# Log-softmax over 8192 rows of 50000: a loop of 62 rounds over eight buffers in place of straight code

## The chip, the cores and the metric

One core of a Trainium2 chip. The metric is the device time of one execution in microseconds (us). "Before" is the kernel given, "changed" the one after the edit. Executions come in a fast and, now and then, a slow state; fast ones are compared with fast ones.

## The reference

```python
x: (16, 512, 50000) float32
max_x   = max(x, axis=-1)
shifted = x - max_x
out     = shifted - log(sum(exp(shifted), axis=-1))
```

Each element is read once and written once: 1638.4 MB in, 1638.4 MB out.

## The kernel before

A tile is 16 rows of the input. Each row is cut into 8 pieces, so that a tile fills 128 partitions with 6250 elements each (3.2 MB); there are 512 tiles. Eight tile buffers of 25000 bytes per partition lie in SBUF, the on-chip memory. Python unrolls everything: the program is one straight line of 512 copies.

```python
G = 8; R = P // G; EXP_C = 3125; NBUF = 8; AHEAD = 7

data = ctx.enter_context(tc.tile_pool(name="data", bufs=NBUF))
...
def load(t):
    buf = data.tile([P, W], FP32, name="buf")
    nc.sync.dma_start(out=buf, in_=xt[t])              # issued from SP
    tiles[t] = buf

def front(t):
    nc.vector.reduce_max(out=pmax, in_=buf, axis=AX)   # DVE, 6.7 us
    ...                                                # DVE: maximum across the 8 pieces, 4 short ops
    for j in range(nexp):                              # ACT: two exponentials with row sums
        nc.scalar.activation(out=dump, in_=buf[:, j * EXP_C : (j + 1) * EXP_C],
            func=ACT.Exp, bias=negmax[:, 0:1], scale=1.0, accum_out=part[:, j : j + 1])
    for j in range(nexp):                              # PE: sum across the 8 pieces
        nc.tensor.matmul(rowsum, ones, part[:, j : j + 1], start=j == 0, stop=j == nexp - 1)
    nc.scalar.activation(out=logsum, in_=rowsum, func=ACT.Ln)

def back(t):
    nc.vector.tensor_scalar(out=buf, in0=buf, scalar1=shift.pop(t)[:, 0:1],
        scalar2=logs.pop(t), op0=ALU.add, op1=ALU.subtract)     # DVE, 3.5 us
    nc.scalar.dma_start(out=ot[t], in_=buf)            # issued from ACT

for t in range(AHEAD):
    load(t)
for t in range(ntiles + 1):
    if t < ntiles:
        front(t)
    if t >= 1:
        back(t - 1)
    if t + AHEAD < ntiles:
        load(t + AHEAD)                                # waits for the store that frees the buffer
```

## Time and profile before

| | before |
|---|---|
| time, median of 3 (lowest, highest) | 7614.08 us (7613.85, 7614.22) |
| data moved | 432 GB/s in nearly every slice |
| DVE / ACT / PE busy | 73% / 41% / 8% |
| load, issue to landing | 51.9 us |
| store, issue to landing | 37.5 us |
| instruction fetch packets on the page | 68 + 16 |

The page of a profile has the busy share of each engine in 40 slices of the span, a row DMA with the share of the 16 DMA engines, and a row GB/s. A line of a group gives the source line, the engine, the operation, what it writes and reads, the count, then the busy time and mean, then the idle time before it and who ended it. The prediction below shows these lines.

### The profile page before, as it was taken

How to read it: one execution, taken by the hardware profiler on the slowest of the kernel's cores; microseconds unless marked ns; L12 is line 12 of the kernel's file. 1: busy time of each engine (PE TensorE's matmuls, PEld its weight loads, DVE VectorE, ACT ScalarE, POOL GpSimd, SP SyncE). 2: the span in 40 equal slices, each digit the busy share in tenths (PEclk: the TensorE clock that was granted, in tenths of full speed). 3: DMA queues.
4: the chain of work that ended last, by engine and by line, in shares of the span. 5: the costliest groups of instructions: out<-in, count | busy, mean ns of one | idle time of the engine just before them, and what ended most of it. 6: DMA issues, size and time to landing. Idle time of an engine off the chain costs nothing.

```text
span 7612.6 us, 12833 instructions
## 1 busy us (share of the span) xinstructions
PE 600.6 (8%) x2048; PEld 513.2 (7%) x2048; DVE 5567.2 (73%) x3072; ACT 3153.1 (41%) x2561; POOL 1.2 (0%) x7
## 2 busy tenths in 40 slices
PE   0000000000000000000000000000000000000000
PEld 0000000000000000000000000000000000000000
DVE  7777777777777777777777777777777777777776
ACT  4444444444444444444444444444444444444443
POOL 0000000000000000000000000000000000000000
DMA  9999999999999999999999999999999999999998
GB/s 425 433 432 432 432 432 432 432 432 432 432 432 432 432 432 432 432 432 432 432 432 432 432 432 432 432 432 432 432 432 432 432 432 432 431 432 432 432 432 380
DMA packets 147540, 3277.68 MB, mean 431 GB/s; under 512 B 16384, under 2 KB 16384, under 8 KB 16384
## 3 DMA queue, kind: packets, MB, share of 16 engines
q1 hardware_dynamic: 73728, 1638.43, 50.0%
q10 hardware_dynamic: 73728, 1638.43, 50.0%
q14 instruction: 68, 0.56, 0.0%
q8 instruction: 16, 0.26, 0.0%
HBM read 1638.40 MB, written 1638.40 MB: 430 GB/s over the span
## 4 chain that ended last, share of the span: by engine, by line
DVE 73%; another core or an unknown queue 25%; issue 1%; DMA 0%; ACT 0%; PE 0%; ACTq 0%
DVE pmax L81 45%; DVE buf L117 23%; DVE allmax L84 1%; DVE rowmax L86 1%; DVE spread L91 1%; DVE negmax L96 0%; DMA buf<-in_x_dram 0%; ACT dump L102 0%; PE rowsum L108 0%; ACT logsum L112 0%; ACTq L102 0%
## 5 line engine op out<-in xcount | busy, mean ns | idle before, releaser
L81 DVE TENSOR_REDUCE pmax<-buf 128x1 f32<-128x6250 f32 x512 | 3411.8, 6664 | 1953.7 <-DMA buf<-in_x_dram 1953.7
L102 ACT ACTIVATE dump<-buf,negmax 128x3125 f32<-128x3125 f32 x1024 | 2938.1, 2869 | 4092.9 <-DVE negmax L96 4029.5
L117 DVE TENSOR_SCALAR buf<-buf,negmax,logsum 128x6250 f32<-128x6250 f32 x512 | 1789.7, 3496 | 4.5 <-ACT logsum L112 3.6
L108 PE MATMUL rowsum<-part,ones 128*128 128x1 f32 x2048 | 600.6, 363 | 6991.7 <-ACT dump L102 6991.7
L108 PEld LDWEIGHTS rowsum<-part,ones 128*128 128x128 f32 x2048 | 513.2, 311 | 7079.0 <-ACT dump L102 7057.2
L112 ACT ACTIVATE logsum<-rowsum 128x1 f32<-128x1 f32 x512 | 87.6, 171 | 345.8 <-PE rowsum L108 345.8
L102 ACT ACTIVATION_READ_ACCUMULATOR dump<-buf,negmax 128x1 f32 x1024 | 191.1, 187 | 0.0
L96 DVE STREAM_TRANSPOSE negmax<-spread 128x32 f32<-128x32 f32 x512 | 108.2, 211 | 17.7
L84 DVE STREAM_TRANSPOSE allmax<-pmax 128x32 f32<-128x32 f32 x512 | 108.3, 211 | 17.4
L86 DVE TENSOR_REDUCE rowmax<-allmax 128x4 f32<-128x32 f32 x512 | 95.3, 186 | 17.7
L91 DVE COPY spread<-rowmax 128x32 f32<-128x32 f32 x512 | 92.9, 181 | 17.8
L67 ACT ACT_TABLE_LOAD x1 | 1.3, 1283 | 0.8 <-PEq L146 0.8
L59 POOL TENSOR_SCALAR_AFFINE_SELECT ones<-ones 128x128 f32<-128x128 f32 x1 | 0.4, 403 | 0.1
L63 POOL TENSOR_SCALAR_AFFINE_SELECT ones<-ones 128x128 f32<-128x128 f32 x1 | 0.4, 397 | 0.1
L57 POOL MEMSET ones<- 128x128 f32 x1 | 0.2, 204 | 0.3 <-POOLq L146 0.3
L146 POOL MEMSET const-bfloat16-1.0<- 128x1 bf16 x1 | 0.1, 101 | 0.0
L146 POOL MEMSET const-uint8-127<- 128x1 uint8 x1 | 0.1, 101 | 0.0
L146 POOL MEMSET const-float32-0.0<- 128x1 f32 x1 | 0.1, 98 | 0.3 <-issue 0.3
L146 POOL MEMSET const-float32-1.0<- 128x1 f32 x1 | 0.1, 98 | 0.0
## 6 DMA issues: line engine op xcount, KB each, us to landing
buf<-in_x_dram SPq DMA_DIRECT2D x512, 3125.0 KB, 51.9
out_dram<-buf ACTq DMA_DIRECT2D x512, 3125.0 KB, 37.5
```

The costliest lines, as they stand in the source:

```text
L59: nc.gpsimd.affine_select(out=ones3, in_=ones3, pattern=[[-G, R], [0, G]], base=0, channel_multiplier=1, compare_op=ALU.is_ge, fill=0.0,)
L63: nc.gpsimd.affine_select(out=ones3, in_=ones3, pattern=[[G, R], [0, G]], base=G - 1, channel_multiplier=-1, compare_op=ALU.is_ge, fill=0.0,)
L67: nc.scalar.preload_act_table_set("natural_log_exp_and_others")
L81: nc.vector.reduce_max(out=pmax, in_=buf, axis=AX)
L84: nc.vector.transpose(out=allmax, in_=pmax.to_broadcast([P, SQ]))
L86: nc.vector.tensor_reduce(out=rowmax, in_=allmax.rearrange("p (r g) -> p r g", g=G), op=ALU.max, axis=AX, negate=True,)
L91: nc.vector.tensor_copy(out=spread.rearrange("p (r g) -> p r g", g=G), in_=rowmax[:, :, None].to_broadcast([P, SQ // G, G]),)
L96: nc.vector.transpose(out=negmax, in_=spread)
L102: nc.scalar.activation(out=dump, in_=buf[:, j * EXP_C : (j + 1) * EXP_C], func=ACT.Exp, bias=negmax[:, 0:1], scale=1.0, accum_out=part[:, ...
L108: nc.tensor.matmul(rowsum, ones, part[:, j : j + 1], start=j == 0, stop=j == nexp - 1)
L112: nc.scalar.activation(out=logsum, in_=rowsum, func=ACT.Ln)
L117: nc.vector.tensor_scalar(out=buf, in0=buf, scalar1=shift.pop(t)[:, 0:1], scalar2=logs.pop(t), op0=ALU.add, op1=ALU.subtract,)
```

## The change

The intent is a short program: one body of eight tiles that runs 62 times, between a first and a last round of straight code. The loop is built without a barrier at the end of each round (`iteration_sync="reg_based"`: the waits compare against counts kept in registers). Since the row numbers are then in registers, the compiler can no longer see that stores touch different rows, so this is declared.

```diff
-    for t in range(AHEAD):
-        load(t)
-    for t in range(ntiles + 1):
-        if t < ntiles:
-            front(t)
-        if t >= 1:
-            back(t - 1)
-        if t + AHEAD < ntiles:
-            load(t + AHEAD)
+    bufs = [data.tile([P, W], FP32, name=f"buf{j}") for j in range(NBUF)]
...
+    def back(j, t, queue=nc.scalar):
...
+        store = queue.dma_start(out=dram(ot, t), in_=buf).ins
+        tc.add_to_no_dep_group("stores", store)
+        tc.declare_no_dep(
+            store, group="stores", across_iterations=True,
+            reason="each tile's rows of the output are written once",
+        )
+
+    def round_of(t, first=False, last=False):
+        for j in range(NBUF):
+            front(j)
+            if first and j == 0:
+                continue
+            back((j - 1) % NBUF, t + j - 1)
+            if j == 0 or not last:
+                load((j - 1) % NBUF, t + j - 1 + NBUF)
+
+    for j in range(NBUF):
+        load(j, j)
+    round_of(0, first=True)
+    with tc.For_i(NBUF, ntiles - NBUF, NBUF, iteration_sync="reg_based") as t:
+        with tc.manual_schedule():
+            round_of(t)
+    round_of(ntiles - NBUF, last=True)
+    back(NBUF - 1, ntiles - 1, queue=nc.sync)
```

(Cut: the pools' sizes, an assertion, and the small tiles, which get fixed names in place of rotating ones: eight each of `negmax` and `logsum`, one for each buffer, two of `part`, one of the others.)

## The prediction

> **What bounds the kernel now.** I read the page's head and slices first, then the DMA queues, the waits, the groups, and last the two ends of the run in stretches.
>
> The slices and the queues:
>
> ```profile
> span 7612.6 us, 12833 instructions
> DMA  9999999999999999999999999999999999999998
> GB/s 425 433 432 432 432 432 432 432 432 432 432 432 432 432 432 432 432 432 432 432 432 432 432 432 432 432 432 432 432 432 432 432 432 432 431 432 432 432 432 380
> ...
> q1 hardware_dynamic: 73728, 1638.43, 50.0%
> q10 hardware_dynamic: 73728, 1638.43, 50.0%
> q14 instruction: 68, 0.56, 0.0%
> q8 instruction: 16, 0.26, 0.0%
> ```
>
> The reader sees a flat 432 GB/s from end to end, half loads and half stores, and two small queues of instruction fetches. No slice has a hole. The groups and waits say that the engines follow the transfers:
>
> ```profile
> L81 DVE TENSOR_REDUCE pmax<-buf 128x1 f32<-128x6250 f32 x512 | 3411.8, 6664 | 1953.7 <-DMA buf<-in_x_dram 1953.7
> L117 DVE TENSOR_SCALAR buf<-buf,negmax,logsum 128x6250 f32<-128x6250 f32 x512 | 1789.7, 3496 | 4.5 <-ACT logsum L112 3.6
> ...
> buf<-in_x_dram SPq DMA_DIRECT2D x512, 3125.0 KB, 51.9
> out_dram<-buf ACTq DMA_DIRECT2D x512, 3125.0 KB, 37.5
> ...
> SPq L75 <- DMA out_dram<-buf: 7305.6, 504, 26.8
> ```
>
> The fullest engine, DVE, works 5567.2 us of 7612.6, 10.87 us in each of 512 tiles, and waits 1953.7 / 507 = 3.9 us a tile for a load. A load's issue waits about 14.5 us (7305.6 / 504) for the store that frees its buffer. So eight buffers go round: 51.9 us to land, some 29 us in the engines, 37.5 us to store, together 8 tiles of 14.85 us. At any time 51.9 + 37.5 = 89.4 us of round trip are in flight; 89.4 / 14.85 = 6.0 tile transfers of 7.4 us each, some 44 us of queued work per DMA engine.
>
> In the single packet records one 25000-byte packet follows the other on an engine every 924.7 ns, and each engine has 8192 of them: 8192 x 0.9247 = 7575 us. The completion writes add 1024 x 0.006 = 6 us. 7581 us is what no order of the same transfers can undercut. The first packet starts about 2.5 us into the span, and some 2 us follow the last, so the floor is about 7586 us. The kernel is 27 us, 0.35%, above it. Where those are shows in stretches of the run:
>
> ```profile
> 3000.00:4000.00 1000.00, 79.20 (x270) 67.68 (x270) 731.05 (x403) 413.36 (x338) 0.00 (x0) 1.00 1.00 432
> ...
> 7535.00:7580.00 45.00, 4.70 (x16) 4.01 (x16) 33.07 (x19) 23.62 (x20) 0.00 (x0) 1.00 0.76 327
> 7580.00:7613.00 33.00, 1.17 (x4) 1.00 (x4) 12.44 (x7) 6.16 (x5) 0.00 (x0) 1.00 0.66 282
> ```
>
> (The last three columns are clock, DMA share and GB/s.) DMA is full in the middle and idle for 0.24 x 45 + 0.34 x 33 = 22 us in the last 77. The semaphore records say why. A tile's 16 increments, one per DMA engine, land within 2 us of each other at the start, but within 32.6 us for the last loads of the steady part, growing evenly; 13 engines are done with their loads 40 us before the last three. So three engines fall behind little by little, a load counts as landed when the slowest has it, and in the tail the others have nothing left.
>
> I looked for what delays them. Around each fetch packet in 3000 to 3260 us the packet chain of one engine slips: by 0.31 us for the fetch itself and about 0.3 us one packet later (small queue q14), by 0.92 and 0.4 us (q8). 62 x 0.63 + 16 x 1.33 is about 60 us. That is the size of three engines behind by some 20 us each, and PE, ACT and DVE are the three large instruction streams. I can't name the DMA engines in the records, so this match is an inference.
>
> **What the Trainium skill says.** (1) "DMA: Bandwidth & Descriptors", section "Where 436 GB/s comes from", puts the ceiling at 435.2 GB/s, from 16 ports. The trace agrees: 432, that is 99.3% of it. (2) The same page, "Why a DMA increments its semaphore by 16 and not by 1": the 16 parts finish independently, and only the full count means landed. The trace agrees, with spreads from 2 to 32.6 us. (3) "Runtime: NRT & Kernel Launch", "Instruction fetch mechanics": instructions stream in blocks by DMA, prefetch is sequential, and a taken branch whose target is outside the two blocks held stalls for a fetch. This trace shows blocks of 16384 bytes (16 in q8, which fits PE's 4096 instructions) and of 8192 bytes (62 in the body of q14); it has no branch to show the rest. (4) "Advanced Engine Details and Errata", "Control Flow Timing": a branch takes about 51 ns, a compare-and-branch about 108 ns. No run yet shows it.
>
> **The change part by part.**
>
> *Buffers and order.* Still eight buffers, and load t+8 still waits for store t, as before in another notation. Eight loads stand in front instead of seven, but before issued its eighth with nothing to wait for as well. Small tiles go from four copies to one; all but one are made and read on DVE alone, in order, and the partial sums keep two copies, read by PE within a microsecond. Cost 0.
>
> *Instructions.* The work of a tile is the same: DVE 6 instructions, ACT 5 and an issue, PE 8, SP an issue. A round of eight tiles adds a branch and register steps per engine. If each wait and each DMA address costs three such steps at 0.1 us (the skill's compare-and-branch as an estimate), DVE with some 3 waits a tile gets 8 x 3 x 0.3 = 7 us a round, against a slack of 8 x 3.9 = 31 us. ACT is 41% busy and has 70 us of slack in a round of 119; SP has nearly all of it. On the path: 0.
>
> *The back edge.* If an engine stalls there for a fetch, I estimate under 10 us: the fetch queues behind data packets of 0.93 us. A stall of S starves the DMA engines only when it outlasts the queued work, 44 us evenly shared, and it is made up from 31 us of slack before the next. A barrier would have needed everything drained; this loop has none. On the path: 0.
>
> *Stores declared independent.* In straight code the compiler sees that stores touch different rows. In a loop their addresses are in registers, so without the declaration each could wait for the one before, 37.5 us from issue to landing against 14.85 us of a tile. With it, stores keep two or three in flight as now. Against the kernel before: 0.
>
> *Fetches.* Straight code fetches each block once: 78 in the steady run. A round holds about 48 instructions on DVE and on ACT, 64 on PE, plus waits and register steps. That should fit in the blocks held, and nearly all fetches disappear. Then the engines stay level, the last load lands earlier by what the slowest engine was late, some 20 us (24 us by another count: the tile takes 14.857 us where 16 packets and two completion writes take 14.81, times 512). The 34.5 us after that landing (7578.0 to 7612.6: maximum, exponentials, last two stores) stay. Stores pushed into the tail give some back; the floor of 7586 also stands in the way. I take 17 us: 7614 - 17 = 7597.
>
> *Tail.* The last store goes out on SP instead of ACT. It waits for the same DVE write, then for the DMA engines. Under 1 us.
>
> **The rivals.**
> 1. *The loop refetches its blocks each round*, since the body crosses a block border or a prefetch of the next block throws out the target. Then 62 rounds x 1 or 2 fetches x 0.63 us = 39 to 78 us on the DMA engine concerned, where there were about 15 to 20. It falls behind faster, and once the queue's 44 us are used up its own total sets the time: plus 20 to 65 us, 7630 to 7680. For it: waits and register steps could double the body, and the skill's account of sequential prefetch. Against it: 48 to 64 instructions are well below a block.
> 2. *The lag is not due to fetches* but belongs to three slower DMA engines. Then nothing moves: 7610 to 7616. Against it: the spacing of packets is 924.7 ns on all of them, with no slower group.
> 3. *The loop's waits are coarser than the straight code's*: loads or stores that wait for an older transfer on the same semaphore (there are eight DMA semaphores for six transfers in flight), or for all of an earlier round. Two transfers fewer in flight would be hidden, since 44 us are queued where a few are needed; a complete drain each round would cost a refill of some 40 us x 62 = 2500 us. The words "without barriers" speak against it.
> 4. *DVE becomes the bound*: it needs 4 us more a tile, 32 us a round. No counted cost comes near.
>
> **Range and chances.** Base case 7597 at about 0.55; no change, 7613, at 0.2; refetching at 0.15; coarser waits at 0.1, mostly above 7680. The weighted middle is about 7602 us. Eight times in ten between 7585, the floor, and 7650. Faster by 2% would be 7462, below the floor of 7586: 0.01, for an error of mine in that floor. Slower by 2% is over 7766, only through rival 3: 0.06. Within 2%: 0.93.
>
> **What would show it.** Right: 432 GB/s in every slice, the same DVE wait of about 3.9 us a tile for loads, instruction packets down from 84 to some 30 or fewer, the landing spread of loads near 2 to 10 us up to the end, and less idle DMA in the last 77 us. Rival 1: instruction packets in the hundreds. Rival 2: few instruction packets, but a spread that still grows to 30 us. Rival 3: DMA below 9 in the slices at regular distances, SP waiting for loads or ACT's queue for stores. What would make me wrong most: holes in the DMA row once a round.

## The result, and the profile after

The changed kernel takes 7645.64 us in the median of 6 runs, five of them from 7644.98 to 7646.1 (median 7645.45) and one slow one of 7816.88; before took 7614.15 beside it. The ratio of the fast runs is 1.0041 (95% interval 1.0028 to 1.0054). Ratios here are the mean time of one kernel's fast runs over that of the other's of the same rounds, so not quite the ratio of the medians quoted. That is 31 us slower: inside the range and within 2%, but on the other side of 7614 from the base case of 7597.

The only profile of this first set fell into the slow execution. It shows 432 GB/s up to about 5250 us and about 403 from there on; that is not explained here and nothing rests on it. The profile below is of the first experiment, the same kernel once more, in a fast run of 7645.29 us.

Page of the changed kernel, slices and queues:

```profile
span 7643.6 us, 21938 instructions
...
DMA  9999999999999999999999999999999999999997
GB/s 423 433 431 433 431 433 431 433 431 433 431 433 431 431 432 432 432 432 432 432 432 432 432 432 432 432 432 431 432 432 432 432 432 432 432 432 432 432 432 309
...
q14 instruction: 5, 0.04, 0.0%
q8 instruction: 1, 0.02, 0.0%
```

The reader sees the same flat 432 GB/s, fetches down from 84 packets to 6, and one slice that differs: the last falls to 309, where before had 380.

The waits (engine, line, what ended the wait, total us, times, longest us):

```profile
DVE pmax L87 <- DMA buf<-in_x_dram: 1843.2, 485, 10.8
...
DVE pmax L87 <- PEq L168: 82.0, 1, 82.0
DVE pmax L87 <- SPq L138: 41.3, 1, 41.3
```

DVE waits for loads as before, 3.8 us a tile. New are two waits that happen once each: 41.3 us on the way into the loop (at 101 to 142 us) and 82.0 us on the way out (at 7454 to 7536 us). L138 is the loop's line; L168 is only the line from which the kernel is called.

Stretches of the same profile (us, then PE, PEld, DVE, ACT, POOL busy, clock, DMA share, GB/s):

```profile
100.00:145.00 45.00, 1.17 (x4) 1.00 (x4) 3.74 (x2) 3.85 (x5) 0.00 (x0) 1.00 1.00 428
...
3000.00:4000.00 1000.00, 78.85 (x270) 67.57 (x270) 733.15 (x403) 413.77 (x338) 0.00 (x0) 1.00 1.00 432
7440.00:7490.00 50.00, 1.75 (x6) 1.50 (x6) 10.88 (x6) 8.02 (x8) 0.00 (x0) 1.00 1.00 432
7490.00:7536.00 46.00, 0.00 (x0) 0.00 (x0) 0.40 (x1) 0.00 (x0) 0.00 (x0) 1.00 0.59 234
7536.00:7644.00 108.00, 9.37 (x32) 8.00 (x32) 89.46 (x49) 49.25 (x40) 0.00 (x0) 1.00 0.71 297
```

The entry costs next to nothing: DVE stands, but the DMA engines have queued work (428 GB/s). In the middle DVE is busy 733 us of 1000, where before it was 731: the loop itself adds nothing that shows. At the exit the engines stand from 7454 us. The DMA engines live on queued work up to 7490; then they idle for 0.41 x 46 = 19 us. From 7536 to the end, DVE does the last eight tiles at 10.9 us each with hardly a load left to issue, and the DMA engines idle for 0.29 x 108 = 31 us more. Together 50 us, where the last 77 us of before had 22.

The two kernels' packet records give the same account for a DMA engine as a whole. Between its first and its last packet, 59.3 us are left over beside 8192 packets of 924.7 ns, their completion writes and the fetches, against 26.4 before; and fetches take some 2 us less. 33 - 2 = 31 us is the whole difference. Of the 33 us, 28 are idle time at the exit (50 - 22). The other 5 are longer packets: 929.3 ns in the mean against 928.7, times 8192 (a packet's record overlaps the next one's by some 3 ns). Most of that, 3.5 us, falls after 7440 us, again at the exit.

The program that was built says what the engines wait for at the exit (names shortened):

```text
SP   end of loop: branch  [waits for all 8 DMA semaphores, DVE, ACT, PE]
DVE  end of loop: branch  [waits for the barrier's release]
ACT  end of loop: branch  [waits for the barrier's release]
```

There is no barrier in a round, but there is one behind the last. It waits for every load and store under way. The trace agrees: SP goes through waits for these semaphores until 7535.1 us, the last load lands at 7534.9, and DVE starts again at 7535.6.

Transfers, issue to landing:

```profile
buf<-in_x_dram SPq DMA_DIRECT2D x512, 3125.0 KB, 24.0
out_dram<-buf ACTq DMA_DIRECT2D x511, 3125.0 KB, 59.3
```

Before had 51.9 and 37.5. Nearly the same number of transfers is under way, but now most of them are stores. A reason that fits, not tested: at the entry all eight buffers were full and DVE then worked through them at 10.9 us a tile, faster than the 14.85 us that the DMA engines take, so stores piled up.

### The profile page after: what moved, and what is told of

It reads as the page before. It is cut to its first block, busy times and chain, and to the rows that moved or that the text cites. A ratio compares the mean times of both kernels' runs of the same rounds, so it can differ in the third digit from the quotient of the medians.

```text
span 7815.1 us, 21938 instructions
## 1 busy us (share of the span) xinstructions
PE 598.3 (8%) x2048; PEld 512.7 (7%) x2048; DVE 5576.5 (71%) x3072; ACT 3152.9 (40%) x2561; POOL 1.2 (0%) x7
## 2 busy tenths in 40 slices
DMA packets 147462, 3276.92 MB, mean 419 GB/s; under 512 B 16384, under 2 KB 16384, under 8 KB 16384
## 6 DMA issues: line engine op xcount, KB each, us to landing
out_dram<-buf SPq DMA_DIRECT2D x1, 3125.0 KB, 12.5
```

## The experiments

Theory A: the rounds are free, and the time is lost once, at the exit. Theory B: each of 62 back edges costs half a microsecond. A second question was whether fetches make DMA engines late, as the prediction had it. Every kernel below gave correct results. In the runs with several rounds before took 7614.1 us (lowest 7613.8, highest 7616.1).

**1. The changed kernel again.** No edit.

> The changed kernel once more, since its only profile fell into a slow execution (7816.9 us against 7645.6). Theory A, the loop's exit: the loop itself is as good as the straight code or better, and the time is lost once, where the engines leave the loop, wait for every transfer to land and then do the last eight tiles with nothing left to load. Time 7645 within 2; a fast profile shows DMA full (432 GB/s) until about 7500 us; the semaphores of a load land within 10 us of each other to the end; and 45 to 60 us of DMA time are idle in the last 170 us. Theory B, the rounds: 31 us over 62 rounds, half a microsecond for each back edge. Then the idle DMA time is spread over the run, and the tail looks like that of the kernel before (22 us idle).

Measured: 7645.24 us (7644.82 to 7647.91), ratio 1.0042 (1.0025 to 1.0059). The profile above is this run's. DMA is full to 7490 us and the idle time lies in the tail, which is A. A branch of the loop (below for DVE, in ns: shortest, median and longest) takes 61 ns on DVE, 49 on ACT, 54 on SP and 220 on PE, 63 times each, which leaves nothing of B.

```profile
L138 DVEq COMPARE_BRANCH  x63: 55/61/74, 97.8 to 7450.2; - x63
```

The loads' semaphores landed within 6.3 us of each other to the end, as expected. The stores' did not, which I had not asked about: 15 parts of a store near 7300 us land within 10 us of the first, the sixteenth after 36.1 us. One DMA engine is late although nothing is fetched between 110 and 7467 us.

That late engine matters at the exit. The parts of the last four stores before it that land last come at 7477.8, 7492.6, 7507.4 and 7522.2 us; the other 15 parts had landed by 7451.3, 7466.1, 7480.9 and 7495.7. Each frees a buffer for one of the last loads, so these are issued some 26 us later than 15 of 16 engines would allow, and the barrier waits for them.

**2. Two loops in a row.** One exit and one entry more, at half time.

```diff
-    with tc.For_i(NBUF, ntiles - NBUF, NBUF, iteration_sync="reg_based") as t:
-        with tc.manual_schedule():
-            round_of(t)
+    half = 32 * NBUF
+    for lo, hi in ((NBUF, half), (half, ntiles - NBUF)):
+        with tc.For_i(lo, hi, NBUF, iteration_sync="reg_based") as t:
+            with tc.manual_schedule():
+                round_of(t)
```

> The loop is cut in two at half, one right after the other: one exit and one entry more, the same rounds. Theory A: one more drain in the middle, 15 to 25 us of DMA idle while everything lands, some 20 more until stores and loads flow again: 7645 + 40 = 7685, between 7670 and 7700, with one hole in the DMA row at half time. Theory B: the same number of back edges less one, 7645 within 3.

Measured: 7670.64 us (7667.44 to 7698.16), ratio 1.0086 (1.0068 to 1.0105). That is 25 us more than one loop, at the low end of what A expected, and B falls: there is one back edge fewer. Stretches around half time:

```profile
3700.00:3800.00 100.00, 5.86 (x20) 5.00 (x20) 54.02 (x30) 30.78 (x25) 0.00 (x0) 1.00 1.00 432
3800.00:3880.00 80.00, 2.32 (x8) 2.01 (x8) 26.31 (x13) 12.31 (x10) 0.00 (x0) 1.00 0.64 267
3880.00:3980.00 100.00, 10.52 (x36) 9.01 (x36) 98.54 (x55) 55.41 (x45) 0.00 (x0) 1.00 1.00 428
```

The hole is 0.36 x 80 = 29 us of idle DMA; after it the DMA engines are full at once, so the refill that I had put at some 20 us costs little. The drain also makes the DMA engines level again: the parts of a store land within 17 us of each other ahead of it, within 2 us in the 100 us after it, and within 20 us again at the end.

**3. Four buffers.** `NBUF = 4`, so 126 rounds of four tiles.

> Four buffers in place of eight: 126 rounds of four tiles. Theory A: after the exit four tiles are left instead of eight, so 4 x 10.9 + 14 = 58 us of engine work beside 4 x 7.4 = 30 us of stores, 28 us idle instead of about 48: 7645 - 20 = 7625, between 7612 and 7635, if four buffers still keep the DMA engines full (4 x 14.85 less 29 us in the engines leaves 30 us for two transfers that need 7.4 us each). Theory B: twice as many back edges, 7645 + 31 = 7676.

Measured: 8246.62 us (8244.85 to 8255.67), ratio 1.083. A miss of both theories, by an error of my own:

```profile
buf<-in_x_dram SPq DMA_DIRECT2D x512, 3125.0 KB, 16.9
out_dram<-buf ACTq DMA_DIRECT2D x511, 3125.0 KB, 16.5
```

I had taken 7.4 us for a transfer. Beside another one it takes 16 to 17 us. 16.9 + 16.5 + some 30 us in the engines are 63 us for four tiles, or 16 us a tile, where the DMA engines need 14.85; measured are 8246 / 512 = 16.1. Four buffers starve the DMA engines, and the run tells nothing of the exit. It does say what eight are for.

**4. The exit one round earlier.** Two rounds of straight code behind the loop.

```diff
-    with tc.For_i(NBUF, ntiles - NBUF, NBUF, iteration_sync="reg_based") as t:
+    with tc.For_i(NBUF, ntiles - 2 * NBUF, NBUF, iteration_sync="reg_based") as t:
         with tc.manual_schedule():
             round_of(t)
+    round_of(ntiles - 2 * NBUF)
```

> The loop ends one round earlier and two rounds stand behind it as straight code. Theory A: the exit costs its drain (some 40 us, as in the two loops) in a place where loads are still to come, and the end has the tail of straight code with level DMA engines (about 12 us above the floor of 7586): 7638, between 7625 and 7655. It says whether the exit is dear for its drain or for the last eight tiles. Theory B: one back edge fewer, 7645.

Measured: 7632.48 us (7631.61 to 7641.58), ratio 1.0024 (1.0007 to 1.0041): 13 us less than the changed kernel. A had expected a gain of this kind (7638), B none for one back edge less. Its profile is of the slowest of the four runs. The stretches at the exit and at the end:

```profile
7360.00:7430.00 70.00, 0.00 (x0) 0.00 (x0) 4.11 (x1) 0.00 (x0) 0.00 (x0) 1.00 0.58 239
7430.00:7500.00 70.00, 7.03 (x24) 6.00 (x24) 69.03 (x42) 37.86 (x31) 0.00 (x0) 1.00 0.82 343
...
7560.00:7640.00 80.00, 5.02 (x18) 4.24 (x18) 43.75 (x25) 24.80 (x21) 0.00 (x0) 1.00 0.97 415
```

The drain is dear (0.42 x 70 + 0.18 x 70 = 42 us), but with loads still to come the end itself is nearly full. So the exit costs its drain wherever it stands, and at the very end the eight tiles without loads on top. The drain is longer here than in experiment 2 (29 us); in this profile two engines, not one, land stores some 37 us late ahead of the exit (table below).

**5. Without the declaration.** The lines with `add_to_no_dep_group` and `declare_no_dep` removed.

> Without the declaration that the stores are independent. If it matters as I said, each store of the loop waits for the store before to land. A store alone then needs at least 7.4 us[...], and 14.8 us when it shares the DMA engines with loads, so a tile takes 15 to 18 us: 7900 to 9200 us, with ACT's queue waiting for stores. If the order of transfers on one queue makes the wait free, 7645.

Measured: 9409.48 us (one run, so its state is unknown), a little above the range expected. Waits and transfers:

```profile
DVE buf L112 <- ACT logsum L108: 3619.6, 493, 7.9
...
ACT dump L100 <- DMA out_dram<-buf: 524.2, 44, 12.1
...
out_dram<-buf ACTq DMA_DIRECT2D x511, 3125.0 KB, 18.2
```

9409 / 512 = 18.4 us a tile, which is the 18.2 us of one store from issue to landing: one store at a time. ACT, which issues the stores, is held behind them, and DVE then waits for ACT's logarithm. The declaration is worth 1764 us to the loop, and nothing against the kernel before, as predicted.

**6. A barrier in each round.** `iteration_sync` left at its default.

> The same loop with the default barrier at each back edge. Theory A makes it 62 exits: each round drains and refills, some 40 us each: 7645 + 61 x 40 = 10100 us, between 9300 and 11000, with a hole in the DMA row in every round. If a drain cost next to nothing in mid-run, it would stay below 7800.

Measured: 8903.9 us (one run, so its state is unknown), below the range expected. (8903.9 - 7645.2) / 61 = 20.6 us for each barrier, half of the 40 that I had given a drain. The page's row and the wait:

```profile
GB/s 426 356 386 351 390 352 358 385 351 391 350 361 381 350 391 352 367 375 351 391 350 373 370 350 390 350 379 363 351 391 351 385 357 351 390 351 391 351 354 360
...
DVE pmax L87 <- PEq L138: 3189.7, 61, 67.7
```

DVE stands 52 us at each barrier (3189.7 / 61), but 44 us of queued transfers and a quick restart hide more than half. Here nine in ten transfers have their semaphores within 1.8 us of each other, so 20.6 us is a drain without a late engine. The difference to the 25 us of experiment 2 fits the lateness there.

**7. A long body.** Two iterations of 31 rounds.

```diff
+    body = 31 * NBUF
-    with tc.For_i(NBUF, ntiles - NBUF, NBUF, iteration_sync="reg_based") as t:
+    with tc.For_i(NBUF, ntiles - NBUF, body, iteration_sync="reg_based") as t:
         with tc.manual_schedule():
-            round_of(t)
+            for k in range(31):
+                round_of(t + k * NBUF)
```

> Two iterations of a body of 31 rounds in place of 62 iterations of one: the same order of tiles, one entry, one exit, but the instructions are fetched again as in straight code (more of them, with the register steps: some 100 fetch packets against 12). Tests the other half of my account, that fetches make three DMA engines late. If they do: the semaphores of the last loads land 20 to 35 us apart instead of under 10, and the exit waits for the late engines: 7645 + 15 to 25 = 7660 to 7670. If the lag has another cause: under 10 us apart and 7645 within 3.

Measured: 7669.93 us in the median of four, one of them slow (7792.49). The three fast runs, 7665.67 to 7672.9, have the median 7666.96; ratio 1.0073 (1.0053 to 1.0093). That is 22 us more than the changed kernel, as expected of fetches. Fetches, and a stretch late in the run:

```profile
q14 instruction: 117, 0.96, 0.0%
q8 instruction: 22, 0.36, 0.0%
...
6000.00:7000.00 1000.00, 78.54 (x268) 67.10 (x268) 734.46 (x408) 414.13 (x336) 0.00 (x0) 1.00 1.00 430
```

Two DMA engines more are late (table below), and DMA falls from 432 to 430 GB/s late in the run. By the packet records the engines hardly idle there (0.2 us in these 1000 us); their packets take longer, 933 ns in the mean against 929 in 1000 to 2000 us. That the late engines' lag has outgrown the queue and holds the others up is inferred: the last part of a store lands 41 us after the first from 4000 us on, and no later. One part of the expectation missed: it is the stores, not the loads, that land far apart.

**8. Straight code with fewer instructions.** One exponential and one matrix multiplication a tile.

```diff
-EXP_C = 3125
+EXP_C = 6250
-            dump = dump_pool.tile([P, EXP_C], FP32, name="dump")
+            dump = dump_pool.tile([P, EXP_C], mybir.dt.float8e4, name="dump")   # in SBUF; it is never read
```

(Cut: the pool of `dump` moves from PSUM to SBUF, and the activation gets `saturate=False`.)

> The straight kernel of before with one exponential over 6250 elements and one matrix multiplication for each tile in place of two (the discarded exponentials go to one-byte elements in SBUF[...]; the row sum is still taken in fp32). PE's instructions halve (16 fetches to 8), ACT's fall by 40%. If the lag comes from fetches, the spread of the last loads falls from 32 us, by a fifth to a half, and the time by 3 to 10 us, to 7604 to 7611. If not, 7614 within 1. The values stay correct.

Measured: 7612.01 us (7611.43 to 7612.18), ratio 0.9997 (0.998 to 1.0013). PE's fetches fell from 16 to 8 and q14's packets from 68 to 60; the spread of the last loads fell from 32 to 27 us. The direction is as expected, the size is smaller than the range, and by the interval it is the same time.

**9. Straight code with more fetches.** Each pair of matrix multiplications three times.

```diff
-        for j in range(nexp):
-            nc.tensor.matmul(
-                rowsum, ones, part[:, j : j + 1], start=j == 0, stop=j == nexp - 1
-            )
+        for again in range(3):
+            for j in range(nexp):
+                nc.tensor.matmul(
+                    rowsum, ones, part[:, j : j + 1], start=j == 0, stop=j == nexp - 1
+                )
```

> The straight kernel of before with each pair of matrix multiplications done three times over (the same result; PE goes from 8% to some 24% busy, off the path: it adds about 2.3 us to a chain that has that much slack in the waits for loads). PE's fetches of 16384 bytes go from 16 to 48. If fetches make a DMA engine late at 1.33 us each, one engine loses 43 us more than before, beyond the some 44 us of queued work that hide a lag: spread of the last loads 50 us and more, DMA below 432 GB/s in the second half, and the time up by 15 to 45 us, to 7630 to 7660. If fetches don't matter to the time: 7614 within 3.

Measured: 7629.36 us (7623.44 to 7630.0), ratio 1.0018 (1.0003 to 1.0033): 15 us more, just under the range expected. Page, waits and stretch:

```profile
q8 instruction: 48, 0.79, 0.0%
q14 instruction: 68, 0.56, 0.0%
...
DVE pmax L81 <- DMA buf<-in_x_dram: 1957.8, 506, 11.1
DVE buf L118 <- ACT logsum L113: 12.5, 6, 5.3
...
6000.00:7000.00 1000.00, 192.89 (x804) 181.44 (x804) 731.06 (x403) 412.43 (x335) 0.00 (x0) 1.00 1.00 430
```

0.5 MB of instructions more cost up to 15 us beside 3277 MB of data, since one engine seems to carry them. The rival is the longer work of PE in each tile. It can have made little of it: DVE waits for ACT's logarithm, which follows PE, only in the first 175 us and the last 75 us (12.5 us in all, before 3.6), and in between for loads alone. By tile 500 DVE is already 11.7 us later than before (7426.4 us against 7414.7); the other 3 us, of the tail, may be PE's. Again DMA falls to 430 GB/s late. The spread didn't rise to 50 us as expected; it stayed at 29, with the rate reduced instead.

How late each engine is, near 7300 us (from the semaphore records: time of the 13th to 16th part of a transfer after its first; averages over some tiles):

```text
                              loads                      stores
before                        5.8  23.5  28.5  32.2      0.6  10.8  15.7  19.4
changed (1)                   1.1   1.3   1.4   6.2      6.0   8.7  10.0  36.1
exit earlier (4), near 7220   2.3   6.9  15.7  24.4      2.5   5.1  37.0  37.7
long body (7)                 6.7   7.3   8.0  11.5     10.2  23.2  38.1  41.7
straight, one exponential (8) 2.7  16.0  27.2  27.4      1.7   8.4  19.6  19.8
straight, more fetches (9)    8.0   9.8  12.9  29.2      7.4   8.4   9.2  24.7
```

With the usual number of fetches three engines are late, with more in the long body again three, in the changed kernel one. This fits fetches as the cause of two of the three, and something else of one. But experiment 4, with as few fetches as the changed kernel, has two. They fall behind most between 2500 and 3000 us, where 252 packets take over 950 ns (8 to 101 in each other 500 us before the exit), and nothing here explains that. So the number of late engines in one profile is weak evidence; that fetches cost time rests on the times of experiments 7 and 9. In experiment 9 only one engine stands out, and its lag stops growing at 29 us from some 4800 us on; that it then holds the others up is inferred.

In the changed kernel's packet records the packets of one engine come 14.82 to 14.87 us apart from tile to tile (starts at 3021.10, 3035.95, 3050.77 and 3065.64 us), those of the other 15 engines 14.81, with no fetch near. These 0.04 us a tile would make some 20 us over 500 tiles, as an estimate. What delays the engine stays open, and whether this is the whole of its lag was not shown.

**10. A shorter tail.** Experiment 8, with the last two stores issued from SP and the last tile subtracted and stored in two halves.

> An attempt to beat both: the straight kernel with one exponential for each tile (run before: 7612), and a shorter tail. The last two stores go out on SP, so that the second last no longer waits behind the last tile's exponentials on ACT (3.4 us late in the profile of before), and the last tile is subtracted and stored in two halves. 7612 - 6 = 7606, between 7602 and 7610. If the end is set by the late DMA engines alone and not by these waits: 7612 within 1.

Measured: 7612.34 us (7610.67 to 7612.54), ratio 0.9997 (0.9985 to 1.001). A miss: no gain over experiment 8. By the second reading named there, the late DMA engines set the end, not these waits; no further run tested that. No version tried beats the kernel before clearly.

## Why the prediction was right or wrong

The time lay inside the range and "within 2%" held. The reason for the narrow range, a kernel at its floor of transfers, held. The small shift inside it went the wrong way, and that 7646 still lay under 7650 was partly luck: the cases foreseen above 7616 were refetching and coarser waits, neither occurred, and the loss that did occur was not among them.

- **The bound** held: 423 to 433 GB/s in every slice but the last.
- **Instructions and back edge, "on the path: 0"**, held for the rounds: 61 ns for a branch, DVE busy 733 against 731 us in 1000, no holes.
- **The step that failed is the back-edge step's last sentence, "A barrier would have needed everything drained; this loop has none. On the path: 0."** It is true of the rounds and false of the exit. I counted the loop's turns and forgot that a loop is also left. Linked to it is "The 34.5 us after that landing (...) stay". After the barrier 108 us follow, since none of the last eight tiles had been begun. The exit makes at least 28 of the 33 us that each DMA engine loses.
- **Fetches**: 84 packets became 6, as expected. "Then the engines stay level" was wrong by one engine: its stores land 36 us apart. I had read three late engines as three instruction streams; experiments 7 and 9 show that fetches do cost time (22 us, and 12 to 15), experiment 1 that they are not all of the lag. The gain of 17 us did not come: from the start of tile 100 on DVE to that of tile 500 the loop takes 5940.5 us and the straight code 5943.8, which fits one late engine setting nearly the pace that three had set. The loads did get level, but the loop's end is not set by the loads' landing alone: it waits for the stores too, and those carry the lag.
- **Stores declared independent** held, and experiment 5 put 1764 us on it.
- **Rival 3** used 40 us for a drain; experiment 6 measured 20.6.
- **Rival 1**, refetching each round, did not occur. **Rival 2** was half right: the lag is partly not due to fetches, but the spread of loads fell, and the time moved, by the exit.
- **Buffers and order, "cost 0"**: the order held, the balance did not. Loads land in 24.0 us instead of 51.9, stores in 59.3 instead of 37.5. No cost of that in the middle shows.
- **Slips in its numbers**, which change nothing here: all 68 fetches of q14 on the page lie in the span, so 62 should be 68, 78 should be 84, and "about 60 us" is 64; of the last load the first 13 parts land 29 to 42 us before the last three; `negmax` and `logsum` go to eight copies, not to one; and a weighted mean of the four cases is 7617 or more, so 7602 can only be meant as a median.

## What to carry to other kernels

When a kernel sits at its transfer floor, look at its ends: a loop without barriers between its rounds still has an entry and an exit, and the exit may drain everything. Ask at each of the two places what is still queued for the DMA engines: the entry here was free with eight loads queued, and the exit was dear with none to come. A shorter program saves instruction fetches, which share the DMA engines with the data, but here that was worth less than one drain.

## What the Trainium skill lacked or had wrong

- "Runtime: NRT & Kernel Launch", section "Instruction fetch mechanics": it calls a block's cost mostly hidden. Where the DMA engines are full it isn't: with 32 more blocks for PE the kernel took 15 us more, some 12 of them ahead of its tail (experiment 9). Two block sizes show, 16384 bytes and 8192 bytes; the page has one.
- "Advanced Engine Details and Errata", section "Control Flow Timing": it gives about 108 ns for a compare-and-branch. Measured in the loop: 61 ns on DVE, 49 on ACT, 54 on SP, 220 on PE.
- "DMA: Bandwidth & Descriptors", section "Where 436 GB/s comes from": it says that for transfers with HBM the HBM side, about 358 GB/s, binds. By its own working that is half of a stack shared by two cores; as a rule for any one core it doesn't hold. One core here moved 432 GB/s, half of it reads and half writes.
- "DMA: Bandwidth & Descriptors", section "Why a DMA increments its semaphore by 16 and not by 1": it has that the 16 parts finish independently, not that the lag of an engine builds up over a long run, to 32 to 42 us here, and is wiped out by a drain (from 17 us to under 2).
- None of the pages that I read has the cost of a loop's barrier or exit where transfers bound: 20.6 us a barrier, 25 us for one more exit in mid-run.
